# A two-layer hybrid trunk on one core: inputs laid out feature-major, the first loads reordered, the long convolution's taps in other proportions and its rows last in the projection

## The chip, the core and the metric

One core of a Trainium2 chip runs the whole program in one launch. The metric is device time in microseconds (us); the median of 3 runs of the kernel before is 2325.66 us (2324.86 to 2325.68).

## What is computed

Two layers of a decoder trunk for 256 prompt positions and 8 sample positions (264 columns in all), model width 2048, float32 in and out. Per layer:

```
z  = rmsnorm(x) @ W_in                       # columns for the groups A, B, C, D
ya = b * conv3(c * x~)                       # A: short causal convolution, taps aw, with a past state
yb = rmsnorm_head(GLA(q, k, v, log a)) * silu(r)             # B: gated linear attention, with a state
yc = silu(layernorm(conv31(glu(c1, c2)) + cb))               # C: depthwise, 31 taps cw, with a past state
yd = u * (tril(W_s) @ layernorm(gelu(v)) + b_s)              # D: spatial gating
x  = x + concat(ya, yb, yc, yd) @ W_o
x  = x + (silu(h @ W_gate) * (h @ W_up)) @ W_down            # h = rmsnorm(x), d_ff 5632
```

and a last rmsnorm. Outputs are y for prompt and sample, and the new states of the convolutions, of the GLA and of D.

## The kernel before

Everything is held feature-major: features on the 128 partitions, the 264 tokens as columns. `xs` is the residual in 16 k-tiles of 128x264; `split_x` makes from it, times the norm's gain, a high part `xh` (fp32r) and a rest `xl`. Each weight matrix is walked by `stream`: for a group of 512 output columns, k-tiles come in **chunks** of two (KC = 2). A chunk is one DMA of 512 KB into `raw` (4 buffers), a cast by ScalarE to `wh` (L293), a subtraction by VectorE to `wl` (L294; `wh` and `wl` have 3 buffers), and 4 x 2 x 3 = 24 matmuls of 264 columns on TensorE (L308 `xh`,`wh`; L309 `xl`,`wh`; L310 `xh`,`wl`). A 2048-row group is 8 chunks, 192 matmuls. In the mixer the groups run in the order c2, c1, r (528 columns), q, v, vd, u, ac, ax, ab, then four groups of the projection w_o; then the feed-forward network (FFN) runs w_gate, w_up and w_down.

Around the change:

- **Opening.** `x_prompt` lies token-major in HBM. It is loaded in four DMAs into `xp` and turned by TensorE: per k-tile two transposes of `xp` (L343) and one of the sample rows `xd` (L344) into `ps_x`, then a copy to `xs` by ScalarE (L346) or VectorE (L348). The gain is loaded as 4 rows and transposed too (L139). All of the first loads are issued by SyncE, in the order of the code: a quarter of x, the gain, the sample rows, two chunks of weights, a quarter of x, two chunks, the rest of x.
- **Small weights.** `load_rows` (L118) loads the per-feature vectors as 53 rows of 512; `prep_params` (L144) transposes them (L147) to `par`. `prep_state` transposes the past states of the two convolutions (L164, L174) and folds them into `accs` and `accA`. The spatial weights `sgr` are masked, transposed to `wst` (L469), and their first entries spread by a matmul (L472). In layer 0 this happens on GpSimd's DMA queue and in the program after c1; for layer 1 the parameters and states are loaded by SyncE and turned within layer 0's FFN.
- **The long convolution (C).** `conv_all` yields 4 x (1 + 30 + 1) = 128 steps: per 128 features one ScalarE start, 30 VectorE taps (L482, 128x256) and one tap for the samples. `step_back`, called once a chunk, issues as many steps as a rate says: 1.5 a chunk for 16 chunks, then 2.5. When the steps are used up, `fin_c` runs the LayerNorm over `cc` (its reductions by TensorE, its chain by VectorE), Silu on ScalarE (L503, with a table load) and `emit_y(8)`, which makes `yh8` (L382) and `yl8` (L383): the C rows of w_o's input.
- **The projection.** `order` (L829) says in which order its 16 k-tiles are used: D (12 to 15), B (4 to 7), C (8 to 11), A (0 to 3). The A rows `yah`, `yal` (L822, L823) are made from the group before, ab.

The instructions of each engine stand in an order that a scheduler fixes at build time; each engine runs its own in that order.

## Time and profile before

| what | value |
|---|---|
| median of 3 runs | 2325.66 us |
| the profiled execution | 2325.71 us |
| its span in the trace | 2323.8 us |
| TensorE (PE) busy | 2293.6 us, 99% |
| VectorE (DVE) busy | 1414.0 us, 61% |
| ScalarE (ACT) busy | 1019.2 us, 44% |
| DMA, mean rate | 177 GB/s |
| TensorE idle, waiting for `yh` | 11.1 us, in 2 waits |

The profiled execution is 0.05 us from the median of the runs, so sums are made against 2325.71. A matmul row's duration covers its whole way through the array, and rows overlap: what a matmul costs is the distance between the starts of neighbours. Idle time of an engine is only lost where the engine is the one that sets the end.

### The profile page before, as it was taken

How to read it: one execution, taken by the hardware profiler on the slowest of the kernel's cores; microseconds unless marked ns; L12 is line 12 of the kernel's file. 1: busy time of each engine (PE TensorE's matmuls, PEld its weight loads, DVE VectorE, ACT ScalarE, POOL GpSimd, SP SyncE). 2: the span in 40 equal slices, each digit the busy share in tenths (PEclk: the TensorE clock that was granted, in tenths of full speed). 3: DMA queues.
4: the chain of work that ended last, by engine and by line, in shares of the span. 5: the costliest groups of instructions: out<-in, count | busy, mean ns of one | idle time of the engine just before them, and what ended most of it. 6: DMA issues, size and time to landing. Idle time of an engine off the chain costs nothing.

```text
span 2323.8 us, 44164 instructions
## 1 busy us (share of the span) xinstructions
PE 2293.6 (99%) x18656; PEld 2271.3 (98%) x18656; DVE 1414.0 (61%) x2076; ACT 1019.2 (44%) x1302; POOL 71.1 (3%) x138
## 2 busy tenths in 40 slices
PE   9999999999999999999999999999999999999997
PEld 8999989999999999999999998999999999999997
DVE  6699966555655555444467998565555555554444
ACT  5644444444444444444345444444444444434333
POOL 3101000000000000000020100000000000000000
PEclk9999999999999999999999999999999999999999
DMA  8446545555555555555574555555555555555553
GB/s 243 146 155 183 172 153 187 182 181 181 180 189 182 182 182 182 179 178 180 182 202 149 174 172 169 162 179 180 181 181 189 182 182 181 182 181 174 177 177 129
DMA packets 208874, 412.44 MB, mean 177 GB/s; under 512 B 14001, under 2 KB 14067, under 8 KB 208644
## 3 DMA queue, kind: packets, MB, share of 16 engines
q1 hardware_dynamic: 204644, 400.53, 54.1%
q0 software_dynamic: 4032, 9.09, 1.5%
q8 instruction: 146, 2.39, 0.4%
q14 instruction: 52, 0.43, 0.1%
HBM read 404.25 MB, written 6.29 MB: 177 GB/s over the span
## 4 chain that ended last, share of the span: by engine, by line
PE 97%; ACT 2%; DVE 0%; issue 0%; DMA 0%; SPq 0%; DVEq 0%; ACTq 0%
PE pw L308 23%; PE pw L309 23%; PE pw L310 23%; PE pwx L308 8%; PE pwx L309 8%; PE pwx L310 8%; PE ps_lv L597 1%; PE ps_os L705 0%; ACT s L701 0%; ACT wh L293 0%; DMA raw<-in_w_in_dram 0%; PE ps_y L870 0%; ACT cc L503 0%; PE ps_sv L774 0%; PE ps_o L667 0%
## 5 line engine op out<-in xcount | busy, mean ns | idle before, releaser
L294 DVE TENSOR_TENSOR wl<-raw,wh 128x1024 fp32r<-128x1024 f32 x752 | 918.8, 1223 | 763.7 <-ACT wh L293 763.0
L293 ACT ACTIVATE wh<-raw 128x1024 fp32r<-128x1024 f32 (+1 forms) x752 | 795.7, 1060 | 1219.5 <-PE pw L309 694.2
L308 PE MATMUL pw<-xh,wh 128*128 128x264 f32 x3136 | 889.4, 286 | 1.9 <-ACT wh L293 1.7
L309 PE MATMUL pw<-xl,wh 128*128 128x264 f32 x3136 | 887.4, 285 | 0.0
L310 PE MATMUL pw<-xh,wl 128*128 128x264 f32 x3136 | 874.0, 285 | 0.1
L308 PEld LDWEIGHTS pw<-xh,wh 128*128 128x128 f32 x3136 | 590.2, 189 | 3.8 <-ACT wh L293 2.4
L309 PEld LDWEIGHTS pw<-xl,wh 128*128 128x128 f32 x3136 | 590.7, 188 | 2.3 <-issue 1.7
L310 PEld LDWEIGHTS pw<-xh,wl 128*128 128x128 f32 x3136 | 583.7, 189 | 6.9 <-issue 4.0
L308 PE MATMUL pwx<-xh,wh 128*128 128x264 f32 x960 | 272.9, 285 | 0.0
L310 PE MATMUL pwx<-xh,wl 128*128 128x264 f32 x960 | 272.2, 284 | 0.0
L309 PE MATMUL pwx<-xl,wh 128*128 128x264 f32 x960 | 272.1, 284 | 0.0
L309 PE MATMUL pw<-hl,wh 128*128 128x264 f32 x880 | 250.6, 285 | 0.0
L308 PE MATMUL pw<-hh,wh 128*128 128x264 f32 x880 | 250.1, 285 | 0.0
L310 PE MATMUL pw<-hh,wl 128*128 128x264 f32 x880 | 248.7, 285 | 0.0
L308 PEld LDWEIGHTS pwx<-xh,wh 128*128 128x128 f32 x960 | 180.8, 188 | 0.1
L310 PEld LDWEIGHTS pwx<-xh,wl 128*128 128x128 f32 x960 | 180.8, 188 | 0.0
L309 PEld LDWEIGHTS pwx<-xl,wh 128*128 128x128 f32 x960 | 180.5, 188 | 0.0
L308 PEld LDWEIGHTS pw<-hh,wh 128*128 128x128 f32 x880 | 165.8, 188 | 0.0
L309 PEld LDWEIGHTS pw<-hl,wh 128*128 128x128 f32 x880 | 165.7, 188 | 0.0
L310 PEld LDWEIGHTS pw<-hh,wl 128*128 128x128 f32 x880 | 165.1, 189 | 0.1
L309 PE MATMUL pwx<-hl,wh 128*128 128x264 f32 x528 | 150.7, 285 | 0.0
L308 PE MATMUL pwx<-hh,wh 128*128 128x264 f32 x528 | 150.2, 285 | 0.0
(311 smaller groups left out, 2259.9 us busy)
## 6 DMA issues: line engine op xcount, KB each, us to landing
raw<-in_w_gate_dram SPq DMA_DIRECT2D x176, 512.0 KB
raw<-in_w_up_dram SPq DMA_DIRECT2D x176, 512.0 KB
raw<-in_w_down_dram SPq DMA_DIRECT2D x176, 512.0 KB
raw<-in_w_in_dram SPq DMA_DIRECT2D x144, 512.0 KB
raw<-in_w_o_dram SPq DMA_DIRECT2D x64, 512.0 KB
raw<-in_w_in_dram SPq DMA_DIRECT2D x16, 528.0 KB
xp<-in_x_prompt_dram SPq DMA_DIRECT2D x4, 512.0 KB
...
```

The lines of the kernel that those rows point to most:

```text
L293: actf(wh[:, :, :ncol], r[:, :, :ncol], AF.Copy)
L294: sub = tt(out=wl, in0=r[:, :, :512], in1=wh[:, :, :512].bitcast(F32), op=ALU.subtract)
L308: mm(out=o, lhsT=a, rhs=rh[kk], start=first, stop=False)
L309: mm(out=o, lhsT=a, rhs=rl[kk], start=False, stop=False)
L310: mm(out=o, lhsT=wl[:, j, m * P:(m + 1) * P], rhs=rh[kk], start=False, stop=last)
L597: mm(out=pl[:, g * P:(g + 1) * P], lhsT=pm[:, q, blk(Tb)], rhs=qd[:, q, :, Tb * 64:Tb * 64 + 64], start=True, stop=True)
```

## The change

**Layout.** The host lays x, the per-feature vectors, the taps, the spatial weights and a second copy of the convolution states out feature-major, so each loads straight into place; x_prompt is padded to 264 columns. The transposes of x, of the gain, of the parameters, of the states and of the spatial weights leave the program, with the copies behind them. `par` now takes 11 loads of 128 short rows (8 to 496 bytes a partition).

**First loads.** SyncE issues the gain, then x in pieces of 2, 2, 4, 4, 4 k-tiles with the sample columns and chunks 2 and 3 of the weights between them; ScalarE issues chunk 0 (in two halves) and chunk 1. Chunk 0 is cast and subtracted in halves. Five small copies bring the sample columns from `xd` into `xs`. In both layers the other small loads (`small_loads`, and in layer 0 the parameters and states too) are issued after the first evacuation of c2.

**Taps and rows.** The rate is 3 steps a chunk for 8 chunks, 2.25 for 8, then 2.5. The C rows stand last in w_o's order, the A rows third.

```diff
-        back.append((conv_all(), fin_c, chain(repeat(1.5, 16), repeat(2.5))))
+        back.append((conv_all(), fin_c, chain(repeat(3, 8), repeat(2.25, 8), repeat(2.5))))
...
-        order = [o + i for o in (12, 4, 8, 0) for i in range(4)]
+        order = [o + i for o in (12, 4, 0, 8) for i in range(4)]
...
-        with tc.high_priority():
-            for i in range(4):
-                dma(out=xp[:, :, i * 512:(i + 1) * 512],
-                    in_=x_prompt[0, :, i * 512:(i + 1) * 512].rearrange("(t p) d -> p t d", p=P))
...
-        for k in range(KT):
-            ps = psm("ps_x")
-            for t in range(2):
-                transpose(ps[:, t * P:(t + 1) * P], xp[:, t, k * P:(k + 1) * P], ident)
-            transpose(ps[:, 256:264], xd[:, k * P:(k + 1) * P], ident[:NS, :NS])
...
+    with tc.high_priority():
+        xd = cst.tile([P, KT, NS], F32, tag="xd", name="xd")
+        adma = nc.scalar.dma_start
+
+        def load_x(k0, k1):
+            dma(out=xs[:, k0:k1, :], in_=x_prompt[:, k0:k1])
+
+        def load_w0(i, dma):
+            early.append(load_w(w_in[0], D_MODEL, COL["c2"], 512, i * KC, dma, KC if i == 0 else 1))
+
+        gain0 = load_gain(0)
+        load_w0(0, adma)
+        load_x(0, 2)
+        dma(out=xd, in_=x_sample)
+        load_w0(1, adma)
+        load_x(2, 4)
+        load_w0(2, dma)
+        load_x(4, 8)
+        load_w0(3, dma)
+        load_x(8, 12)
+        load_x(12, 16)
+        for k0, k1 in ((0, 2), (2, 4), (4, 8), (8, 12), (12, 16)):
+            nc.vector.tensor_copy(xs[:, k0:k1, NPT:], xd[:, k0:k1])
...
+        seen = mt("seen", [P, 1])
+        with tc.issue_after(nc.gpsimd.tensor_copy(seen, sgm[:, 0, 0:1]).ins):
+            if st is None:
+                par = load_params(l, sdma)
+                pasts = [mt("past", [P, 512], tag=tag) for tag in ("att", "t5", "t4")]
+                for i in range(3):
+                    load_state(l, i, pasts[i], sdma)
+            small_loads()
         win(COL["c1"], 512, ev_c1)
         if st is None:
-            par = prep_params(l, load_rows(l, sdma))
             build_masks()
             st = acc_tiles(l)
-            for i, tag in enumerate(("att", "t5", "t4")):
-                past = mt("past", [P, 512], tag=tag)
-                load_state(l, i, past, sdma)
-                prep_state(par, i, past, *st)
+            for i in range(3):
+                prep_state(par, i, pasts[i], *st)
...
-        psW = psm("ps_ws")
-        for h in range(H):
-            transpose(psW[:, h * P:(h + 1) * P], sgr[:, h, :], ident)
-        actf(wst.rearrange("p h i -> p (h i)"), psW, AF.Copy)
-        psw0 = psm("ps_w0")
-        mm(out=psw0[:, :H], lhsT=ones_s[0:1, :], rhs=wst[0:1, :, 0], start=True, stop=True)
```

How the instructions stand is shown at three places. The first is TensorE's opening, before (`pw` are the accumulators of the group c2):

```order
L343 MATMUL ps_x<-ident,xp 128x128 x2
L139 MATMUL ps_gain<-ident,grow 128x4 x4
L343 MATMUL ps_x<-ident,xp 128x128 x2
L344 MATMUL ps_x<-ident,xd 128x8 x2
L343 MATMUL ps_x<-ident,xp 128x128 x2
L344 MATMUL ps_x<-ident,xd 128x8
L343 MATMUL ps_x<-ident,xp 128x128 x2
L344 MATMUL ps_x<-ident,xd 128x8
L308 MATMUL pw_261<-xh,wh 128x264
L308 MATMUL pw_262<-xh,wh 128x264
L308 MATMUL pw_263<-xh,wh 128x264
L308 MATMUL pw_264<-xh,wh 128x264
```

and with the change, where line numbers have moved by one (L309, L310, L311 are the three matmuls):

```order
L309 MATMUL pw_165<-xh,wh 128x264
L309 MATMUL pw_166<-xh,wh 128x264
L309 MATMUL pw_167<-xh,wh 128x264
L309 MATMUL pw_168<-xh,wh 128x264
L310 MATMUL pw_165<-xl,wh 128x264
L311 MATMUL pw_165<-xh,wl 128x264
L309 MATMUL pw_165<-xh,wh 128x264
L310 MATMUL pw_166<-xl,wh 128x264
L311 MATMUL pw_166<-xh,wl 128x264
```

The 52 transposes ahead of and between the first matmuls are gone; the first instruction is a matmul of the stream.

The second is VectorE at the start of layer 0's projection, before. The four `wl` rows are the projection's chunks 4, 5, 6 and 7 (counted from 0), between them stands the end of the LayerNorm of C, and TensorE wants `yl8` in chunks 4 and 5:

```order
L294 TENSOR_TENSOR wl_3722<-raw_3719,wh_3721 128x1024
L190 TENSOR_TENSOR sqg_3352<-sqg_3352,rsl_3360 128x264
L191 SCALAR_TENSOR_TENSOR rsl_3360<-sqg_3352,rsl_3360 128x264
L192 TENSOR_TENSOR sqg_3352<-sqg_3347,rsl_3360 128x264
L294 TENSOR_TENSOR wl_3752<-raw_3749,wh_3751 128x1024
L193 TENSOR_TENSOR sqg_3352<-sqg_3352,rsl_3360 128x264
L194 SCALAR_TENSOR_TENSOR sqg_3352<-sqg_3352 128x264
L195 SCALAR_TENSOR_TENSOR rsl_3360<-sqg_3352,rsl_3360 128x264
L428 TENSOR_TENSOR cc_913<-cc_913,rsl_3360 128x1056
L294 TENSOR_TENSOR wl_3782<-raw_3779,wh_3781 128x1024
L383 TENSOR_TENSOR yl8_3376<-cc_913,yh8_3375 128x1056
L294 TENSOR_TENSOR wl_3812<-raw_3809,wh_3811 128x1024
```

and with the change, from the last chunk of the group ab (`wl_3439`) on; `wl_3485`, `wl_3515` and `wl_3545` are the projection's chunks 0, 1 and 2, and TensorE wants `yal` in chunks 4 and 5 and `yl8` in chunks 6 and 7:

```order
L294 TENSOR_TENSOR wl_3439<-raw_3436,wh_3438 128x1024
L434 TENSOR_TENSOR cc_796<-cc_796,rsl_2994 128x1056
L294 TENSOR_TENSOR wl_3485<-raw_3482,wh_3484 128x1024
L820 TENSOR_TENSOR ya_2629<-ya_2629,pw0_3222 128x264
L820 TENSOR_TENSOR ya_2629<-ya_2629,pw1_3223 128x264
L294 TENSOR_TENSOR wl_3515<-raw_3512,wh_3514 128x1024
L820 TENSOR_TENSOR ya_2629<-ya_2629,pw2_3224 128x264
L383 TENSOR_TENSOR yl8_3010<-cc_796,yh8_3009 128x1056
L820 TENSOR_TENSOR ya_2629<-ya_2629,pw3_3225 128x264
L822 TENSOR_TENSOR yal_3221<-ya_2629,yah_3220 128x264 x2
L294 TENSOR_TENSOR wl_3545<-raw_3542,wh_3544 128x1024
L822 TENSOR_TENSOR yal_3221<-ya_2629,yah_3220 128x264 x2
```

`yl8` stood behind the `wl` of chunk 6, two chunks after the first that reads it; now it stands behind that of chunk 1, five chunks ahead of the first that reads it. The end of its LayerNorm stood among chunks 3 to 6 and now stands ahead of chunk 0.

The third is GpSimd's queue in layer 0, before, in which the loads for the attention and the spatial gating come ahead of the states and the parameters:

```order
L393 DMA a_243<-in_gla_a_dram 16x256 x2
L395 DMA sgr<-in_sg_w_dram 128x4x128
L397 DMA sgb<-in_sg_b_dram 128x512
L403 DMA s_239<-in_state_gla_dram 64x4x128 x2
L403 DMA s_240<-in_state_gla_dram 64x4x128 x2
L403 DMA s_241<-in_state_gla_dram 64x4x128 x2
L403 DMA s_242<-in_state_gla_dram 64x4x128 x2
L433 MEMSET cext 128x4x30
L156 DMA past<-in_state_conv_c_dram 120x512 x2
L158 DMA past<-in_state_conv_a_dram 16x512
L577 MEMSET pm 128x1056
```

and with the change, from the small copy that starts it on:

```order
L460 COPY seen<-sgm 128x1
L133 DMA par_432<-in_conv_c_w_dram 128x124
L133 DMA par_432<-in_conv_a_w_dram 128x12
L133 DMA par_432<-in_gla_norm_dram 128x4
L133 DMA par_432<-in_conv_c_b_dram 128x4
L133 DMA par_432<-in_ln_c_g_dram 128x4
L133 DMA par_432<-in_ln_c_b_dram 128x4
```

The parameters now come first, behind a copy of `sgm` that waits for the end of the first group; the rest of the eleven, the three states, and only then `a2`, the spatial weights and the GLA state follow.

## Rows read from the trace of the kernel before

**Rows 1.** The page's line of engine totals: busy us, share of the span, instructions.

```profile
PE 2293.6 (99%) x18656; PEld 2271.3 (98%) x18656; DVE 1414.0 (61%) x2076; ACT 1019.2 (44%) x1302; POOL 71.1 (3%) x138
```

**Rows 2.** Busy time by stretch: from:to and its length, then busy us (instructions) of PE, PEld, DVE, ACT, POOL, the granted TensorE clock, the DMA share and GB/s. A stretch inside the feed-forward network.

```profile
500.00:1000.00 500.00, 500.00 (x4116) 499.63 (x4116) 270.89 (x335) 207.32 (x250) 0.00 (x0) 1.00 0.57 182
```

**Rows 3.** Who TensorE waited for, over the whole run: us in total, times, longest.

```profile
PE pw L308 <- ACT yh L382: 11.1, 2, 5.6
PE ps_x L343 <- DMA xp<-in_x_prompt_dram: 5.3, 1, 5.3
PE pw L308 <- ACT wh L293: 1.7, 3, 0.7
```

**Rows 4.** The opening in order of time: start us, duration us, engine, line, what, how often, and the idle time before it with what ended it.

```profile
0.81 0.47 SPq L333 DMA_DIRECT2D xp<-in_x_prompt_dram  x1
2.10 1.30 SPq L269 DMA_DIRECT2D raw<-in_w_in_dram  x2
...
5.28 0.66 PE L343 MATMUL ps_x<-ident,xp 128*128 128x128 f32 x2 [5.28 <-DMA xp<-in_x_prompt_dram]
...
7.48 1.06 ACT L293 ACTIVATE wh<-raw 128x1024 fp32r<-128x1024 f32 x1 [0.80 <-DMA raw<-in_w_in_dram]
...
9.27 1.25 PE L308 MATMUL pw<-xh,wh 128*128 128x264 f32 x4 [0.24 <-ACT xh L215]
...
12.19 1.08 PE L308 MATMUL pw<-xh,wh 128*128 128x264 f32 x4
...
20.85 0.65 PE L308 MATMUL pw<-xh,wh 128*128 128x264 f32 x4
```

**Rows 5.** Busy time by stretch, columns as in rows 2: from the start to the end of the first group, and ten us within it.

```profile
0.00:41.70 41.70, 36.18 (x244) 32.08 (x245) 26.39 (x47) 26.67 (x47) 11.41 (x27) 1.00 0.77 235
...
10.00:20.00 10.00, 10.00 (x60) 8.67 (x59) 8.53 (x17) 8.27 (x15) 0.00 (x0) 1.00 0.92 341
```

**Rows 6.** Groups of VectorE instructions from 0 to 41.7 us: count, busy us, mean ns of one, and idle time before them.

```profile
L294 DVE TENSOR_TENSOR wl<-raw,wh 128x1024 fp32r<-128x1024 f32 x10 | 12.2, 1223 | 5.5 <-ACT wh L293 5.5
L216 DVE SCALAR_TENSOR_TENSOR xl<-xs,gain,xh 128x264 fp32r<-128x264 f32 x16 | 7.4, 485 | 0.8 <-ACT xh L215 0.8
...
L348 DVE COPY xs<-ps_x 128x264 f32<-128x264 f32 x8 | 3.4, 428 | 7.2 <-PE ps_x L344 7.2
```

**Rows 7.** Groups of TensorE instructions over the whole run, columns as in rows 6: the transposes of x.

```profile
L343 PE MATMUL ps_x<-ident,xp 128*128 128x128 f32 x32 | 8.0, 339 | 5.3 <-DMA xp<-in_x_prompt_dram 5.3
...
L344 PE MATMUL ps_x<-ident,xd 8*128 8x8 f32 x16 | 3.6, 237 | 0.0
```

**Rows 8.** The chain of work that ended last, from 60 to 80 us (start us, us, what): the preparation of layer 0's small weights between the stream's matmuls.

```profile
67.69 0.38 PE ps_par L147 x4
68.07 0.97 PE ps_pc L164 x8
...
71.01 0.35 PE ps_pa L174 x4
...
73.24 0.44 PE ps_ws L469 x4
...
76.70 0.31 PE ps_w L472 x2
```

**Rows 9.** In order of time, columns as in rows 4, around the projection of layer 0 (VectorE's last tap and its last part of the A rows, then ScalarE, then TensorE) and, last, TensorE in layer 1.

```profile
275.36 0.47 DVE L482 SCALAR_TENSOR_TENSOR cc<-cext,par,cc 128x256 f32<-128x256 f32 x1
...
291.91 1.11 DVE L823 TENSOR_TENSOR yal<-ya,yah 128x264 fp32r<-128x264 f32 x3
...
302.19 1.28 ACT L503 ACT_TABLE_LOAD   x1
303.49 2.10 ACT L503 ACTIVATE cc<-cc,par 128x264 f32<-128x264 f32 x4
305.62 1.08 ACT L382 ACTIVATE yh<-cc 128x1056 fp32r<-128x1056 f32 x1
...
300.92 0.28 PE L310 MATMUL pw<-yh,wl 128*128 128x264 f32 x1
306.76 1.25 PE L308 MATMUL pw<-yh,wh 128*128 128x264 f32 x4 [5.56 <-ACT yh L382]
...
311.47 0.28 PE L309 MATMUL pw<-yl,wh 128*128 128x264 f32 x1
...
1450.21 1.03 PE L308 MATMUL pw<-yh,wh 128*128 128x264 f32 x3 [5.56 <-ACT yh L382]
```

**Rows 10.** Busy time by stretch, columns as in rows 2: the matmuls behind that wait in layer 0.

```profile
306.70:311.50 4.80, 4.70 (x20) 4.39 (x21) 1.26 (x1) 0.01 (x1) 0.00 (x0) 0.51 0.14 55
```

**Rows 11.** GpSimd's loads of the small weights: one issue in order of time (columns as in rows 4), and DMA issues of a kind with KB each and the median us from issue to landing.

```profile
44.53 0.53 POOL L123 DMA_DIRECT2D prow<-in_gla_norm_dram  x1
...
past<-in_state_conv_c_dram POOLq DMA_DIRECT2D x2, 240.0 KB, 10.5
...
prow<-in_gla_norm_dram POOLq DMA_DIRECT2D x1, 2.0 KB, 6.1
```

**Rows 12.** Busy time by stretch, columns as in rows 2: the groups r, q and v of layer 0.

```profile
65.50:96.60 31.10, 30.86 (x251) 29.19 (x251) 22.00 (x52) 13.82 (x19) 5.10 (x6) 1.00 0.47 140
96.60:122.60 26.00, 25.22 (x199) 24.24 (x198) 18.51 (x31) 21.47 (x40) 0.00 (x0) 1.00 0.45 136
122.60:153.40 30.80, 30.80 (x258) 30.28 (x257) 30.55 (x60) 12.79 (x21) 0.00 (x0) 1.00 0.51 156
```

More of the change, by code (lines that the diff above doesn't have):

```diff
@@ L131, in load_gain @@
     def load_gain(l):
-        g = tmp.tile([4, 512], F32, tag="sq", name="grow")
-        dma(out=g, in_=norm_mix[l].rearrange("(r n) -> r n", r=4))
-        return g
-    def prep_gain(l, g):
-        ps = psm("ps_gain")
-        for t in range(4):
-            transpose(ps[:, t * 4:(t + 1) * 4], g[:, t * P:(t + 1) * P], ident[:4, :4])
-        gain = cst.tile([P, 4, 4], F32, tag=f"gain{l}", name=f"gain{l}")
-        actf(gain.rearrange("p t r -> p (t r)"), ps[:, :16], AF.Copy)
-        return gain
@@ L144, in prep_params @@
-    def prep_params(l, rows):
-        ps = psm("ps_par")
-        for t in range(4):
-            transpose(ps[:, t * NROW:(t + 1) * NROW], rows[:, t * P:(t + 1) * P],
-                                ident[:NROW, :NROW])
-        par = cst.tile([P, 4, NROW], F32, tag=f"par{l}", name=f"par{l}")
-        actf(par.rearrange("p t r -> p (t r)"), ps[:, :4 * NROW], AF.Copy)
-        return par
+        g = cst.tile([P, KT], F32, tag=f"gain{l}", name=f"gain{l}")
+        keep(dma(out=g, in_=norm_mix[l]))
@@ new lines, in load_gain, with load_params, pcol @@
+        return g
+    def load_params(l, dma):
+        par = cst.tile([P, NPAR], F32, tag=f"par{l}", name=f"par{l}")
+        src = dict(cw=conv_c_w[l], aw=conv_a_w[l], gn=gla_norm[l], cb=conv_c_b[l], lcg=ln_c_g[l],
+                   lcb=ln_c_b[l], ldg=ln_d_g[l], ldb=ln_d_b[l], nf=norm_ffn[l], gb=gla_a_bias[l],
+                   fin=norm_final)
+        for n, (o, w) in PAR.items():
+            keep(dma(out=par[:, o:o + w], in_=src[n]))
+        return par
+    def pcol(par, n, i):
+        o = PAR[n][0] + i
+        return par[:, o:o + 1]
@@ L160, in prep_state @@
     def prep_state(par, i, past, accs, accA):
         if i < 2:
-            ps = psm("ps_pc")
-            for t in range(4):
-                transpose(ps[:, t * 120:(t + 1) * 120], past[:120, t * P:(t + 1) * P], ident[:120, :120])
-            pw = tmp.tile([P, 4, 4, 30], F32, tag="sq", name="pw")
-            tt(out=pw, in0=ps[:, :480].rearrange("p (t b k) -> p t b k", t=4, b=4),
-               in1=par[:, :, 0:30].unsqueeze(2).to_broadcast([P, 4, 4, 30]), op=ALU.mult)
+            pw = past[:, :480].rearrange("p (t b k) -> p t b k", t=4, b=4)
@@ L168, in prep_state @@
+            tt(out=pw, in0=pw, in1=pvec(par, "cw")[:, :, 0:30].unsqueeze(2).to_broadcast([P, 4, 4, 30]),
+               op=ALU.mult)
             a = accs[:, :, 4 * i:4 * i + 4]
             nc.vector.tensor_reduce(out=a, in_=pw, axis=mybir.AxisListType.X, op=ALU.add)
-            tt(out=a, in0=a, in1=par[:, :, 35:36].to_broadcast([P, 4, 4]), op=ALU.add)
+            tt(out=a, in0=a, in1=pvec(par, "cb").to_broadcast([P, 4, 4]), op=ALU.add)
         else:
-            psA = psm("ps_pa")
-            for t in range(4):
-                transpose(psA[:, t * 16:(t + 1) * 16], past[:16, t * P:(t + 1) * P], ident[:16, :16])
@@ L175, in prep_state @@
[L175 to L179 removed]
+            pa = past[:, :64].rearrange("p (k t b) -> p k t b", k=2, t=4)
+            aw = pvec(par, "aw")
@@ L181, in acc_tiles, with old_state @@
+            tt(out=accA, in0=pa[:, 0], in1=aw[:, :, 0:1].to_broadcast([P, 4, NS]), op=ALU.mult)
+            tt(out=pa[:, 1], in0=pa[:, 1], in1=aw[:, :, 1:2].to_broadcast([P, 4, NS]), op=ALU.mult)
+            tt(out=accA, in0=accA, in1=pa[:, 1], op=ALU.add)
+    def old_state(l, a, taps):
+        return a[l][0:NS * taps * GW].rearrange("(b t c) -> b t c", b=NS, t=taps)
     def acc_tiles(l):
@@ L264, in hybrid_trunk_kernel, with load_w @@
     early = []
-    def load_w(W, rows, col0, ncol, k0):
+    fresh = [True]
+    def load_w(W, rows, col0, ncol, k0, dma=dma, pieces=1):
         r = raw_p.tile([P, KC, 528], F32, tag="raw", name="raw")
         i = rows * col0 + k0 * P * ncol
-        dma(out=r[:, :, :ncol],
-            in_=W[i:i + KC * P * ncol].rearrange("(p k n) -> p k n", p=P, k=KC))
+        w = W[i:i + KC * P * ncol].rearrange("(p k n) -> p k n", p=P, k=KC)
+        n = KC // pieces
+        for j in range(0, KC, n):
+            dma(out=r[:, j:j + n, :ncol], in_=w[:, j:j + n])
         return r
```

156 lines of the change are left out of this document (74 added, 82 removed).

## The prediction, made before the changed kernel ran

> **What bounds the kernel now.** I read the page's totals first: TensorE is busy 99% of the span [rows 1], so only what TensorE does or waits for can move the time. Then a stretch of the FFN, for its pace: 4116 matmuls in 500 us, 0.1215 us each, at the full granted clock, with VectorE at 54% [rows 2]. The stream needs 18,048 matmuls of that kind, 2193 us; the change leaves them alone. What can go is the other 130 us. Then the table of TensorE's waits [rows 3]: 11.1 us in two waits of 5.6 for `yh`, 5.3 us at the start for x, 1.7 us for casts. Last I looked at the two places themselves: the opening [rows 4 to 6] and the projection of each layer [rows 9, 10].
>
> **The wait in the projection (undone by the new rates and row order).** In layer 0 TensorE starts its last matmul of the B rows at 300.92, and the first of the C rows at 306.76, after 5.56 us of idling for `yh` [rows 9]. What is late is one chain: the last tap of the convolution at 275.36, LayerNorm, a table load at 302.19 (1.28 us), four Silus (2.10), the cast at 305.62 (1.08). Behind it comes a second cost: from 306.70 to 311.50 the granted clock reads 0.51, the 1.2 GHz level [rows 10], and from 306.76 the 19 matmuls up to 311.47 [rows 9] took 4.71 us where 0.1215 each would be 2.31, 2.4 more. Before the fall TensorE had stood idle. From 300.92 plus one matmul to 306.76 are 5.72; so a layer loses 5.7 + 2.4 = 8.1. Layer 1 shows the same wait at 1450.21 [rows 9], so 16.2 in all.
>
> With the change the 128 steps are used up after 51 chunks instead of 58 (16 chunks at 1.5 gave 24, the other 104 need 42; now 8 x 3 + 8 x 2.25 give 42, the other 86 need 35), and in the built order VectorE's last tap stands 10 chunks earlier and `yl8` 5 chunks earlier. A chunk is 24 x 0.1215 = 2.92 us, so 5 chunks are 14.6 us: `yh8` and `yl8` move from about 307 to about 292. The need for them moves the other way, two chunks later, from 301.0 to 306.9. Either part alone would do, the row order just so (5.8 against 5.7); together they leave some 14 us. The A rows take the place: the last of `yal` starts at 291.91 and takes 1.11 [rows 9], and they are needed at 301.0. That is 8 us of slack, and VectorE has less to do there. I take the whole 16.2; at worst the A rows wait instead and half is left, at best 16.4.
>
> **The opening.** TensorE begins at 5.28 with transposes, when the first 512 KB of x have landed; the first matmul of the stream is at 9.27, behind the landing of the first weights at 7.48 [rows 4]; the first group of 192 is done at 41.7 (244 instructions less the 52 transposes) [rows 5]. At 0.1215 each it would need 23.3. The rest is 9.3 of lead, then the transposes put in between (48 on x, 11.6 us of overlapping durations [rows 7]), and the low clock: at 12.19 four matmuls are 0.22 apart, at 20.85 they are 0.12 apart [rows 4], that is the lower and the upper level; ahead of the rise TensorE had done transposes and matmuls with holes.
>
> Now the first matmul needs the gain (8 KB), two k-tiles of x (264 KB) and both halves of chunk 0 (512 KB), 784 KB. Before, 512 KB of x were there at 5.28 and the sample rows, gain and first weights, 584 KB more, at 7.48, 265 KB a us. At that pace 784 KB are there at 5.28 + 272/265 = 6.3. Half a cast (0.53), then the first `xh` (0.5) give a first matmul at 7.3. ScalarE's three new issues (0.65 each by SyncE's [rows 4]) and its table load end at 4.1, under the landing. Add 23.3, add the 2.4 that the low clock cost behind the wait above, add 0.5 for feeding: 33.5, or 8.2 earlier. Feeding holds if VectorE keeps pace: 8 `wl` (1.22) and 16 `xl` (0.485) [rows 6] and twelve additions for the norm at 0.43 to 0.58 make some 23 us against 25.7 of TensorE; the 8 copies of 0.43 are gone, and five copies of the sample columns, each below 0.43, come. DMA moved 341 GB/s in this part [rows 5]; x and four chunks, 4.3 MB, are there by about 18. Bounds: a first matmul at 6.0 and half the clock cost, 30.5 (11.2 earlier); a first matmul no earlier than 9.27 and 3 us of waits for `wl`, 38.0 (3.7 earlier).
>
> The weights of chunks 0 and 1 come from ScalarE's queue. The rows show one issuer and a DMA share of 0.92 [rows 5], so I count only fewer bytes ahead, 2.0 us of the lead. The Trainium skill (DMA: Bandwidth & Descriptors, "Issuing engines are not separate DMA queues") says that transfers from several engines share the same 16 DMA engines and only issue time is saved. By that alone the lead would shrink by the 1.3 us by which the first weights are issued earlier, and the sum below would be 0.7 higher; no row here has two issuers in the opening.
>
> **The small transposes.** Parameters, states and spatial weights cost TensorE 0.38 + 0.97 + 0.35 + 0.44 + 0.31 = 2.45 us of the chain in layer 0 [rows 8]; the same instructions run once more for layer 1, so 4.9 (4.3 to 5.9, if gaps of neighbours or whole durations count). Of ScalarE's copies behind them some stood in front of casts; of the 1.7 us in which TensorE waited for casts [rows 3] I give 0.4 (0 to 1). The loads for layer 1, 12 issues by SyncE instead of 13 within the FFN, cost nothing: four `raw` buffers, 11.7 us of TensorE's work, cover them, and if they did not, it would be an issue of some 0.5 each.
>
> **What it adds.** In r and q VectorE gets 38 taps instead of 22 by the built order, 16 x 0.40 (taps follow one another at that distance) = 6.4 us more, in 57.1 us where it is busy 40.5 [rows 12]. It fits on the sum; but in q TensorE is already short of 0.8 us, waiting for a cast, and in v VectorE is busy 30.6 of 30.8. I take 1.0 for both layers (0 to 5). In layer 0 GpSimd issues parameters and states only after the first group: from 33, 14 issues of 0.53 end at 40.5, and the states land 6.1 to 10.5 later [rows 11], at 46.5 to 51. VectorE wants them behind the `wl` of c1's seventh chunk, which TensorE reaches at 33.5 + 6 x 2.92 = 51 and VectorE one or two chunks ahead, at 45 to 48. So it may stand up to 6 us, with `wl` of the next chunks queued behind; two finished chunks, 5.8 us, cover that. I count it within the 1.0.
>
> **Sum.** 2325.71 - 16.2 - 8.2 - 4.9 - 0.4 + 1.0 = 2297.0. The profiled execution is 0.05 us from the median 2325.66, so the forecast stands for the median: **2297.0 us**, 1.2% less. The forecast's own range is 2291 to 2303. A change under 0.2% (4.7 us) could not be told from none.
>
> **Rivals.**
> - *The opening is fed no faster* (the worst bound above): c2 ends at 38.0 instead of 33.5, 2301.5. For it: VectorE and ScalarE were busy 8.5 and 8.3 of ten us there [rows 5], and the `xl` of the last four k-tiles wait for the last piece of x. Against: their copies from `ps_x` are gone.
> - *VectorE becomes the bound in r, q and v.* If the 6.4 us of taps find no free place, `wl` is late by that in each layer: 2 x 6.4 more, less the 1.0 counted, 2309. For it: 30.6 of 30.8 in v. Against: 9 us free in r, 7.5 in q [rows 12], and the built order gives v 10 taps instead of 14.
> - *The wait does not go, it changes rows.* `yal` or `yl8` still comes late by half of what it was: 2305. Against it are 8 and 14 us of slack.
> - *Slower: the small loads hold everything.* The layer-0 states come last of 14 loads, 11 of them of 128 short rows, down to 8 bytes. If each had to land before the next is issued, at 6.1 for the eleven and 10.5 for the states [rows 11], the last would be there at 33 + 67 + 32 = 132. VectorE stands from 46 on, TensorE runs dry at 52: 80 us lost and 2.4 of low clock, 2379. It is slower than before once TensorE loses more than the 29.7 gained and 4.7, so from a landing at about 52 + 34 = 86. Against: before, loads of this queue were issued 0.5 apart while others were in flight. The Trainium skill (DMA: Bandwidth & Descriptors, Specifications) wants 512 bytes a transfer and says that below this the engine does a read-modify-write; no row here shows loads of 128 such pieces.
>
> **How the numbers follow.** Forecast 0.73, opening 0.09, VectorE 0.11, changed rows 0.04, slower 0.03. The range 2290 to 2308 takes in the forecast's own, the first and third rivals and the nearer half of the second; it leaves out 2309 and beyond, the slower case and a better opening, some 0.15. Faster by over 0.2%: 0.96 (all but the slower case and a part of the second rival in which several waits add up, 0.01); within 0.2%: 0.01; slower: 0.03.
>
> **What would show it.** Right: TensorE's table of waits has no `yh` and no `yal` at the projection, and the granted clock stays at 1.00 there; the first matmul at about 7.3 and c1's first at about 33.5; the projection of layer 0 begins some 12 us earlier than 288.9. Wrong: a new wait for `wl` or `wh` of several us in c1, r or q, above all one that ends with the landing of `past`; or a first group that ends later than 38.

## The result, and the profile of the changed kernel

| | us | ratio to before |
|---|---|---|
| before, median of 4 runs on the same chip | 2325.67 (2324.86 to 2327.01) | |
| changed, median of 4 runs | 2298.49 (2297.37 to 2300.40) | 0.9883 [0.9866, 0.9901] |
| predicted | 2297.0 (2290 to 2308) | |

27.2 us went; 28.7 were predicted. The profiled execution took 2299.30 us, with a span of 2297.3; by spans it is 26.5 less than before.

TensorE first, since it sets the end. The page's totals (busy us, share, instructions) answer to [rows 1]: 96 instructions fewer on TensorE, the transposes of x and gain (52) and twice the 22 small ones. VectorE and ScalarE are as busy as before.

```profile
PE 2275.0 (99%) x18560; PEld 2258.8 (98%) x18560; DVE 1412.3 (61%) x2074; ACT 1015.4 (44%) x1288; POOL 70.8 (3%) x140
```

Who TensorE waited for (us in total, times, longest), against [rows 3]:

```profile
PE pw L309 <- ACT xh L210: 6.5, 1, 6.5
PE pw L309 <- ACT wh L293: 4.1, 4, 2.0
PE ps_y L869 <- DVE xg L846: 0.3, 1, 0.3
```

The two waits for `yh` are gone and no other row of the projection took their place. The 6.5 is the start. The waits for casts grew: four of them, 4.1 us, the longest 2.0, where before three took 1.7, the longest 0.7. One stands in the opening (0.53, at 21.64), one in r of layer 0 (0.85), one in the q group of each layer (0.81 and 1.96).

**The opening** in order of time (start, duration, engine, line, what; then the idle time before it), against [rows 4]:

```profile
0.81 1.52 ACTq L268 DMA_DIRECT2D raw<-in_w_in_dram  x3
...
3.98 0.63 ACT L293 ACTIVATE wh<-raw 128x512 fp32r<-128x512 f32 x1 [0.33 <-DMA raw<-in_w_in_dram]
5.27 0.63 ACT L293 ACTIVATE wh<-raw 128x512 fp32r<-128x512 f32 x1 [0.66 <-DMA raw<-in_w_in_dram]
5.91 0.92 ACT L210 ACTIVATE xh<-xs,gain 128x264 fp32r<-128x264 f32 x2
...
6.47 1.25 PE L309 MATMUL pw<-xh,wh 128*128 128x264 f32 x4 [6.47 <-ACT xh L210]
...
8.89 1.06 ACT L293 ACTIVATE wh<-raw 128x1024 fp32r<-128x1024 f32 x1 [1.53 <-DMA raw<-in_w_in_dram]
...
13.63 1.74 ACT L210 ACTIVATE xh<-xs,gain 128x264 fp32r<-128x264 f32 x4 [1.39 <-DVE xs L350]
```

The first matmul of the stream starts at 6.47 instead of 9.27. Then ScalarE stands twice, 1.53 us for weights to land and 1.39 for a copy of sample columns that stands behind a `wl` on VectorE (12.28 to 13.50). The DMA share is 0.91 from 10 to 20 us (columns as in rows 2, against [rows 5]). TensorE itself is busy in that stretch; its matmuls are 0.22 apart up to 12.4 and 0.12 from there on, though the granted clock reads 1.00. It reads 1.00 in [rows 5] too, so the low clock that the prediction sees in the opening is read from distances, not from that column.

```profile
10.00:20.00 10.00, 10.00 (x75) 10.00 (x75) 9.73 (x22) 8.61 (x18) 0.00 (x0) 1.00 0.91 335
```

**The projection of layer 0**, against [rows 9]:

```profile
274.29 1.28 ACT L502 ACT_TABLE_LOAD   x1
...
278.55 1.07 ACT L382 ACTIVATE yh<-cc 128x1056 fp32r<-128x1056 f32 x1
...
280.16 1.25 DVE L383 TENSOR_TENSOR yl<-cc,yh 128x1056 fp32r<-128x1056 f32 x1
...
283.49 0.77 DVE L822 TENSOR_TENSOR yal<-ya,yah 128x264 fp32r<-128x264 f32 x2
...
290.65 0.28 PE L309 MATMUL pw<-yah,wh 128*128 128x264 f32 x1
...
296.52 0.28 PE L309 MATMUL pw<-yh,wh 128*128 128x264 f32 x1
```

`yl8` is ready at 281.4 and needed at 296.5, the A rows at 284.3 and 290.7: 15 and 6 us of slack. TensorE's matmuls stay 0.12 apart throughout, at a granted clock of 1.00.

**The q group of layer 1**, ScalarE and then TensorE:

```profile
1224.22 0.48 ACT L530 ACTIVATE absy<-ps_pre,par 128x264 f32<-128x264 f32 x1 [0.30 <-DVE mn L529]
1226.07 1.06 ACT L293 ACTIVATE wh<-raw 128x1024 fp32r<-128x1024 f32 x1 [1.37 <-PE pw L310]
1227.04 0.47 ACT L530 ACTIVATE absy<-ps_pre,par 128x264 f32<-128x264 f32 x1
1227.52 1.28 ACT L531 ACT_TABLE_LOAD   x1
...
1229.48 1.28 ACT L532 ACT_TABLE_LOAD   x1
1230.77 0.65 ACT L532 ACTIVATE absy<-absy 128x528 f32<-128x528 f32 x1
1231.32 1.05 ACT L293 ACTIVATE wh<-raw 128x1024 fp32r<-128x1024 f32 x1
1232.39 1.28 ACT L632 ACT_TABLE_LOAD   x1
...
1233.93 4.79 ACT L700 ACTIVATE s<-s,as 128x128 f32<-128x128 f32 x16
1238.63 1.04 ACT L293 ACTIVATE wh<-raw 128x1024 fp32r<-128x1024 f32 x1
...
1239.72 0.39 PE L309 MATMUL pw<-xh,wh 128*128 128x264 f32 x1 [1.96 <-ACT wh L293]
```

Read it by the casts (L293): they start at 1226.07, 1231.32, 1238.63. The middle gap holds two table loads, the last a third table load and sixteen scalings of the GLA state (L700). TensorE has used up its stock of casts and idles 1.96 us. Behind that the granted clock reads 0.50, the 1.2 GHz level, as one stretch shows: 18 matmuls in 3.40 us, where 28 would fit at 0.1215.

```profile
1241.30:1244.70 3.40, 3.40 (x18) 3.40 (x17) 3.02 (x5) 2.04 (x3) 0.00 (x0) 0.50 0.49 154
```

**Where the time went.** Below, the times between the first matmuls of successive groups of the stream, taken from both traces:

| term | before | changed | difference | predicted |
|---|---|---|---|---|
| end of the first group (c2) of layer 0 | 41.72 | 33.75 | -8.0 | -8.2 |
| r of layer 0; r of layer 1; FFN of layer 0 | 31.18; 28.22; 773.30 | 28.79; 27.67; 771.34 | -4.9 | -4.9 small transposes |
| c1 of layer 1 | 23.69 | 23.33 | -0.4 | (-0.4 casts, in no named group) |
| first projection group, layers 0 and 1 | 32.02; 31.91 | 23.44; 23.41 | -17.1 | -16.2 |
| q to ab, layer 0 | 192.26 | 192.66 | +0.4 | +1.0 new costs, with the next row |
| q to ab, layer 1 | 192.22 | 195.34 | +3.1 | |

These sum to -26.9; the other groups add 0.3, and the spans differ by 26.5. Of the 3.1, the q group alone is 2.75 (25.90 to 28.65). Of the 17.1, 0.9 was not the wait: the last reduction of the convolution's LayerNorm (`ps_var`) ran inside the projection before, 0.45 us of TensorE's time a layer, and now runs in ax. So the wait was worth 16.2, and what was added from q to ab is 2.6.

The -4.9 and the -0.4 hide two larger numbers. Four of the transposes of the spatial weights stood in c1 of layer 1 (L469 in the trace before, at 1211.54), and none of the three waits for casts did, so the -0.4 belongs to the transposes. And r of layer 0 carries a new wait: it took 28.79 here, but 27.67 in e3 and e5, which have the same matmuls there and no wait, as r of layer 1 took. So the small transposes were worth 6.4 (3.51 in r of layer 0, where TensorE had waited 0.21 for a cast before, 1.96 in layer 0's FFN, 0.36 and 0.55 in c1 and r of layer 1), and 1.1 was lost again behind a cast that came late because its weights landed late (ScalarE, TensorE, then DMA issues between 40 and 62 us with KB each and median us to landing):

```profile
60.27 1.08 ACT L293 ACTIVATE wh<-raw 128x1056 fp32r<-128x1056 f32 x1 [3.79 <-DMA raw<-in_w_in_dram]
...
61.41 0.39 PE L309 MATMUL pw<-xh,wh 128*128 128x264 f32 x1 [0.85 <-ACT wh L293]
...
raw<-in_w_in_dram SPq DMA_DIRECT2D x6, 528.0 KB, 7.2
s<-in_state_gla_dram POOLq DMA_DIRECT2D x8, 128.0 KB, 8.7
```

Weights took 7.2 us to land there, against 3.8 to 4.0 within the FFN (500 to 1000 us), beside 2.1 MB of GpSimd's small loads, which the change issues behind the first group. That these loads delay the weights is read from the times and was not tried by itself.

### The profile page after: what moved, and what is told of

The parts are those of the page before. It is cut to its first block, busy times and chain, and to the rows that moved or that the text cites. A ratio compares the mean times of both kernels' runs of the same rounds, so it can differ in the third digit from the quotient of the medians.

```text
span 2297.3 us, 43967 instructions
## 1 busy us (share of the span) xinstructions
PE 2275.0 (99%) x18560; PEld 2258.8 (98%) x18560; DVE 1412.3 (61%) x2074; ACT 1015.4 (44%) x1288; POOL 70.8 (3%) x140
## 5 line engine op out<-in xcount | busy, mean ns | idle before, releaser
L294 DVE TENSOR_TENSOR wl<-raw,wh 128x1024 fp32r<-128x1024 f32 (+1 forms) x753 | 920.1, 1223 | 749.2 <-ACT wh L293 748.0
L293 ACT ACTIVATE wh<-raw 128x1024 fp32r<-128x1024 f32 (+2 forms) x753 | 796.2, 1059 | 1206.6 <-PE pw L310 670.7
L309 PE MATMUL pw<-xh,wh 128*128 128x264 f32 x3136 | 891.2, 286 | 10.6 <-ACT xh L210 6.5
L310 PE MATMUL pw<-xl,wh 128*128 128x264 f32 x3136 | 889.5, 285 | 0.0
L311 PE MATMUL pw<-xh,wl 128*128 128x264 f32 x3136 | 876.5, 286 | 0.1
L309 PEld LDWEIGHTS pw<-xh,wh 128*128 128x128 f32 x3136 | 592.0, 189 | 16.1 <-ACT xh L210 6.5
L310 PEld LDWEIGHTS pw<-xl,wh 128*128 128x128 f32 x3136 | 592.2, 189 | 2.2 <-issue 1.7
L311 PEld LDWEIGHTS pw<-xh,wl 128*128 128x128 f32 x3136 | 585.7, 189 | 3.2 <-issue 2.0
L309 PE MATMUL pwx<-xh,wh 128*128 128x264 f32 x960 | 273.1, 284 | 0.0
L311 PE MATMUL pwx<-xh,wl 128*128 128x264 f32 x960 | 272.8, 284 | 0.0
L310 PE MATMUL pwx<-xl,wh 128*128 128x264 f32 x960 | 272.5, 284 | 0.0
L310 PE MATMUL pw<-hl,wh 128*128 128x264 f32 x880 | 250.9, 286 | 0.0
L309 PE MATMUL pw<-hh,wh 128*128 128x264 f32 x880 | 250.3, 285 | 0.0
L311 PE MATMUL pw<-hh,wl 128*128 128x264 f32 x880 | 248.9, 285 | 0.0
L309 PEld LDWEIGHTS pwx<-xh,wh 128*128 128x128 f32 x960 | 181.1, 189 | 0.0
L311 PEld LDWEIGHTS pwx<-xh,wl 128*128 128x128 f32 x960 | 181.0, 189 | 0.0
L310 PEld LDWEIGHTS pwx<-xl,wh 128*128 128x128 f32 x960 | 180.6, 188 | 0.0
L309 PEld LDWEIGHTS pw<-hh,wh 128*128 128x128 f32 x880 | 165.9, 189 | 0.0
L310 PEld LDWEIGHTS pw<-hl,wh 128*128 128x128 f32 x880 | 165.8, 188 | 0.0
L311 PEld LDWEIGHTS pw<-hh,wl 128*128 128x128 f32 x880 | 165.3, 189 | 0.1
L310 PE MATMUL pwx<-hl,wh 128*128 128x264 f32 x528 | 150.7, 286 | 0.0
L309 PE MATMUL pwx<-hh,wh 128*128 128x264 f32 x528 | 150.3, 285 | 0.0
```

The costliest lines, as they stand in the source:

```text
L293: actf(wh[:, j, :ncol], r[:, j, :ncol], AF.Copy)
L294: sub = tt(out=wl[:, j, :], in0=r[:, j, :512], in1=wh[:, j, :512].bitcast(F32), op=ALU.subtract)
L309: mm(out=o, lhsT=a, rhs=rh[kk], start=first, stop=False)
L310: mm(out=o, lhsT=a, rhs=rl[kk], start=False, stop=False)
L311: mm(out=o, lhsT=wl[:, j, m * P:(m + 1) * P], rhs=rh[kk], start=False, stop=last)
```

## The experiments

Each run was timed beside the kernel before on its chip (medians 2325.07 to 2326.45), and is told by its own median; group times are from its one profiled execution. All edits but that of e4 start from the changed kernel.

**1. Rates, rows, or both.** Three kernels take one or both of the tail's edits back (the first edit in e1 and e3, the second in e2 and e3); e4 puts only the tail's edits on the kernel before.

```diff
-chain(repeat(3, 8), repeat(2.25, 8), repeat(2.5))
+chain(repeat(1.5, 16), repeat(2.5))
...
-order = [o + i for o in (12, 4, 0, 8) for i in range(4)]
+order = [o + i for o in (12, 4, 8, 0) for i in range(4)]
```

e1, old rates with the new rows:

> The changed kernel with the old tap rates (1.5, then 2.5 steps a chunk), its new row order kept. Theory (either half of the change covers the wait by itself): the C rows are ready at about the old 306.7 and wanted at 306.9, so at most 0.5 us of waiting a layer, o0 at 23.4 to 24 us instead of 32.0; the group q of layer 1 is no longer short of casts and falls from 28.7 back to 25.9. In all 2296 to 2300 against 2298.5 of the changed kernel. Rival (the rates do the work, the row order nothing): the wait comes back at the later rows, 2 to 6 us of idling and 2.4 of low clock a layer, 2307 to 2315.

Measured 2299.06 (2298.45 to 2303.36), first projection group 25.33. The wait is of the size expected, 0.5 us a layer (the waits of e1, columns as above), but the group is 1.9 longer than 23.4. 0.45 of that is `ps_var`, which is back in the projection. The other 1.5 lie between 295.94 and 298.41, where eight distances of matmuls take 2.47 us instead of 0.97: the wait for `yh`, a cast that ScalarE could run only behind `yh` (0.2 idle), and the first matmuls after each.

```profile
PE pw L309 <- ACT wh L293: 3.6, 6, 1.1
PE pw L309 <- ACT yh L382: 1.0, 2, 0.5
```

e2, new rates with the old rows:

> The changed kernel with the old row order (C rows third, A rows last), its new tap rates kept. Theory: the C rows are ready near 292 on the old clock of layer 0 and wanted at 301, so no wait: o0 at 23.4 us, 2298.5 like the changed kernel, within 1.5. Rival (the row order does the work): the Silu and yh come after the group ab has ended, the wait comes back with 2 to 6 us and the low clock, 2306 to 2315.

Measured 2298.21 (2296.95 to 2299.18), no wait for `yh`, first projection group 23.41: the rates alone remove all of it.

e3, both old:

> The changed kernel with both the old rates and the old row order; layout and loads new. Theory: the wait for yh comes back whole, o0 at 32.0 us in both layers, 17.1 us over the changed kernel, less the 2.7 that q of layer 1 regains: 2313 to 2316. Rival (the wait was due to the transposes and the late loads, not to rates and rows): o0 stays at 23.4, 2296 to 2299.

Measured 2311.85 (2310.93 to 2313.02). The mechanism is as expected: the wait is back at its old size, with the low clock behind it at 292.1 to 298.9 (TensorE in e3, as in rows 9):

```profile
295.67 1.25 PE L309 MATMUL pw<-yh,wh 128*128 128x264 f32 x4 [5.56 <-ACT yh L382]
```

The time is 1 us below the expected range: the first projection groups took 31.31 and 31.36, not 32.0. TensorE's idle time is the same 5.56, but in layer 0 the matmuls behind it were at the low clock for 3.2 us, where before it was 4.8 [rows 10]. With the old rates q of layer 1 is back at 25.94.

e4, the kernel before with the new rates and rows:

> The kernel before with only the two lines of the tail changed (new rates, new row order); layout and loads old. Theory: both waits of 5.6 us and their low clock go, 17.1 us, less up to 2.7 if q of layer 1 loses as in the changed kernel: 2308.5 to 2311.5. If q's loss comes from the new layout, 2308.5 and q at 25.9. Rival (the rates cost VectorE elsewhere what they give here): above 2315.

Measured 2311.92 (2311.36 to 2313.51), 13.7 less than before and a little above the range. The first projection group is 23.5 in layer 0 and 23.4 in layer 1, so the 17.1 are there. Against them stand the q group of layer 0, 1.1 longer behind a wait of 1.90 for a cast, and an opening that ended at 44.11 in the profiled execution, 2.4 later than before, its matmuls 0.22 apart up to 19.4, where before they were 0.12 apart from 15.4 at the latest. Why that came later there I can't say; q of layer 1 stays at 25.91, so the new rates alone do not make it late; the other three runs are 1.2 to 2.2 us shorter. What e3 saves (13.7) and what e4 saves (13.7) sum to 27.4, against 27.2 for the whole change: the tail is half of it, opening and small weights the other half, and within the spread of the runs the two simply add.

**2. What the order and the two issuers of the first loads are worth.** e5 keeps the layout and takes before's order, chunk 0 in one piece, all issued by SyncE (the first part; unchanged lines and the one copy of sample columns less are not shown); e6 only lets SyncE issue the first weights (the second part).

```diff
-fresh = [True]
+fresh = []
...
-early.append(load_w(w_in[0], D_MODEL, COL["c2"], 512, i * KC, dma, KC if i == 0 else 1))
+early.append(load_w(w_in[0], D_MODEL, COL["c2"], 512, i * KC, dma, 1))
...
-gain0 = load_gain(0)
-load_w0(0, adma)
-load_x(0, 2)
-dma(out=xd, in_=x_sample)
-load_w0(1, adma)
-load_x(2, 4)
-load_w0(2, dma)
-load_x(4, 8)
+load_x(0, 4)
+gain0 = load_gain(0)
+dma(out=xd, in_=x_sample)
+load_w0(0, dma)
+load_w0(1, dma)
+load_x(4, 8)
+load_w0(2, dma)
...
-adma = nc.scalar.dma_start
+adma = nc.sync.dma_start
```

> The changed kernel with the feature-major layout kept and the first loads in the order of the kernel before, all issued by SyncE: four k-tiles of x, gain, sample columns, chunks 0 and 1, four k-tiles, chunks 2 and 3, the rest; chunk 0 whole. Theory (layout and order each give a part): 1112 KB stand ahead of the first matmul, as before, so it starts at about 9.0 instead of 6.5; the group c2 ends at 36.3 instead of 33.75, 2301 in all. Rival 1 (the layout alone does it, since the casts of c2 bound it anyway): c2 ends within 0.7 of 33.75, 2298.5 to 2299. Rival 2 (the order does it): c2 ends above 39, 2304 and more.

Measured 2298.88 (2298.76 to 2299.62): first matmul 10.09, end of the first group 35.86 as expected, but the time is 2 us below. In this execution q of layer 1 took 27.13 instead of 28.65, though TensorE's wait there is the same 1.96: the clock did not fall behind it. r of layer 0 was 1.1 shorter as well, without the wait of 0.85. So this run could not tell what the order is worth; e11 does.

> The changed kernel with the weights of chunks 0 and 1 issued by SyncE too, in the order of the code. Theory (only the bytes ahead count): the two halves of chunk 0 and x are issued some 0.8 to 1.5 later, first matmul at 7.3 to 8.0, c2 ends at 34.5 to 35.2, 2299 to 2300. Rival (two issuing engines bring more bandwidth): first matmul above 8.5, c2 ends above 36, 2301 and more. Second rival (issue time was hidden by the data): first matmul at 6.5, no difference.

Measured 2297.62 (2297.13 to 2298.55): first matmul 7.54, 1.1 later than with two issuers, end of the first group 33.20, not later at all. The other traces agree: with one issuer (e6, and e9 and e10 below) the first matmul is at 7.38 to 7.99 and the group ends at 33.20 to 33.84, with two (the changed kernel, e1, e2, e3, e7, e8, e12) at 6.47 to 6.91 and 32.30 to 34.12. A single issuer costs the start and nothing at the end that the spread of executions would show. That is what the Trainium skill says (DMA: Bandwidth & Descriptors, "Issuing engines are not separate DMA queues"): a second issuer saves only the issue time. The trace agrees, with 1.1 us at the first matmul and none at the end of the group.

**3. The late cast in q.** Two suspects: ScalarE's scalings of the GLA state, and VectorE's taps. e7 moves the sixteen scalings to GpSimd (first part); e8 lowers the middle rate (second part).

```diff
-actf(s0[:, j, :], s0[:, j, :], AF.Copy, scale=as_[:, q, b:b + 1])
+nc.gpsimd.tensor_scalar(out=s0[:, j, :], in0=s0[:, j, :], scalar1=as_[:, q, b:b + 1], scalar2=None, op0=ALU.mult)
...
-chain(repeat(3, 8), repeat(2.25, 8), repeat(2.5))
+chain(repeat(3, 8), repeat(1.5, 8), repeat(2.5))
```

> The changed kernel with the sixteen scalings of the GLA state in each layer done by GpSimd instead of ScalarE. Theory (q's waits come from ScalarE, which does the sixteen in one piece of 4.8 us between two casts): no wait of TensorE for wh in q, q at about 24.7 in both layers instead of 25.95 and 28.65, the clock does not fall at 1241, 2292 to 2295. Rival (VectorE's extra taps make q late): q unchanged, 2298.5. Third way: GpSimd is slow or takes VectorE's port, the state comes late to the attention, above 2300.

Measured 2295.81 (2294.34 to 2297.63). 0.8 above what was expected. q is 24.59 and 24.94, better than in either kernel (1.4 and 3.7 less than in the changed one), but the groups v to ab take 1.1 and 1.4 more: the scalings take 15 us on GpSimd (e7, in order of time) where ScalarE took 4.79, and TensorE's table has a new wait of 1.1 us for `vb` at `ps_os` (L704).

```profile
1231.72 15.06 POOL L700 TENSOR_SCALAR s<-s,as 128x128 f32<-128x128 f32 x16 [34.67 <-ACT as L632]
```

> The changed kernel with the rates 3 for eight chunks, 1.5 for eight, then 2.5, that is fewer taps in q (14 in the built order instead of 19). Theory (ScalarE's piece of 4.8 us makes q late): q of layer 1 stays above 28, 2298 to 2299; the last tap comes 4 chunks later, which o0 does not feel (23.4). Rival (VectorE's taps make q late): q of layer 1 falls to 25.9, 2295.5 to 2296.

Measured 2295.96 (2295.47 to 2296.72), q of layer 1 25.94, no fall of the clock: the rival of that run. Either suspect alone, taken away, ends the long wait (e8 keeps 0.75 of it), so neither is the whole cause.

**4. The two remedies together, and the order again.** Three kernels with the middle rate 1.5: with one issuer (e9), with one issuer and the scalings on GpSimd (e10), with the old load order (e11).

> The changed kernel with two edits that were each tried alone: the middle rate 1.5 instead of 2.25, and SyncE instead of ScalarE issuing the first weights. Theory: the gain of the rate (2.5 us: the layer-1 q group 25.9 instead of 28.7) lies at another place than what the issuer does in the opening, so it stays whole, and the issuer is worth nothing at the end of the first group (33.2 to 33.8): 2295.0 to 2296.2. Rival: the issuer's 1.1 us later first matmul costs time after all and was hidden in the earlier run by a luckier q: 2296.5 to 2297.5.

Measured 2296.48 (2294.91 to 2297.99), q 25.94, end of the first group 33.84. It lies 0.3 above the theory's range and at the edge of the rival's; against e8 (2295.96) the issuer is not told from nothing.

> As the run before (middle rate 1.5, SyncE issues the first weights), and the 16 scalings of the GLA state run on GpSimd as well. Theory: both remedies of the late cast in q take away one and the same wait, so together they give no more than the better one in q (24.6 to 25.0), and GpSimd's scalings lengthen v and vd as when they were tried alone (vd about 36): 2294.5 to 2296. Rival: they add up, the second giving another 2.5 us: 2292.5 to 2293.5.

Measured 2293.35 (2292.37 to 2295.34), ratio 0.9862 [0.9847, 0.9877]. The rival of that run holds: they add up, 3.1 below e9 and 2.5 below e7. My theory took the wait for one and the same. But at 25.94 q still holds a wait of 0.75 for a cast, in each layer; without the scalings it is gone and q takes 24.58 in both, and v to ab give back only 0.35 and 0.06, where in e7 they gave back 1.1 and 1.4. That is 2.3 of the 3.1; 0.7 is c1 of layer 1, where TensorE waited 0.51 for a `wl` in e9. Of the kernels run this is the quickest, 5.1 below the changed one.

> The changed kernel with the load order of before (a quarter of x, gain, sample rows, chunk 0 and 1 whole, and so on, all by SyncE; layout feature-major) and the middle rate 1.5, so that the q group of layer 1 doesn't hide what the order is worth. Theory: the new order is worth the 2.1 us at the end of the first group that the profiles showed (35.9 against 33.8), and the earlier run of the old order gave that back by a shorter q (27.1 against 28.7); with q short in both kernels it shows in the time: 2297.5 to 2298.5, the end of the first group at about 35.9. Rival: what the opening gains comes back as a longer r group of layer 0 (28.8 against 27.7), whatever q does: 2295.8 to 2296.8.

Measured 2298.25 (2297.21 to 2299.09), end of the first group 35.30, against 2295.96 in e8 and 2296.48 in e9. The theory holds: the new order, with the halves of chunk 0 and the two issuers that e11 takes back as well, is worth about 2 us (1.8 to 2.3 by the medians); the rest of the opening's 8 is the layout.

**5. Which taps.** In q of the changed kernel VectorE's two `mn` (L529) are parted (in order of time):

```profile
1223.69 0.49 DVE L529 TENSOR_SCALAR mn<-ps_pre,par 128x264 f32<-128x264 f32 x1 [1.39 <-PE ps_pre L528]
1224.10 1.22 DVE L294 TENSOR_TENSOR wl<-raw,wh 128x1024 fp32r<-128x1024 f32 x1
1225.23 0.49 DVE L529 TENSOR_SCALAR mn<-ps_pre,par 128x264 f32<-128x264 f32 x1
```

In e8 they are a pair, and ScalarE has a cast between its two table loads. e12 lowers the rate only for the two chunks in which they run; after r and q 42 steps are done, as in the changed kernel.

```diff
-chain(repeat(3, 8), repeat(2.25, 8), repeat(2.5))
+chain(repeat(3, 8), repeat(1.5, 2), repeat(2.5))
```

> The changed kernel with the rates 3 a chunk for 8 chunks, 1.5 for 2, then 2.5: only the first two chunks of the q group have fewer steps, and after the 16 chunks of r and q 42 steps are done as in the changed kernel. Theory: the wait in the layer-1 q group comes from one place, VectorE's two mn (L529) being parted by a wl, so that ScalarE runs both table loads (L531, L532) ahead of a cast; with the pair together the cast comes 1.2 us sooner: the wait falls from 1.96 to about 0.75, the granted clock stays up, the q group takes 25.9, and the time is 2295.5 to 2297.0 with no fewer taps in q. Rival: it is the number of taps in r and q that makes VectorE late; with 42 again the wait stays near 2.0, the q group takes 27.1 to 28.7 and the time stays 2297.5 to 2299.5.

Measured 2295.42 (2294.67 to 2296.58), ratio 0.9866 [0.985, 0.9883]. ScalarE, VectorE and TensorE in q of layer 1:

```profile
1223.32 0.93 ACT L530 ACTIVATE absy<-ps_pre,par 128x264 f32<-128x264 f32 x2 [0.18 <-DVE mn L529]
1224.27 1.28 ACT L531 ACT_TABLE_LOAD   x1
...
1226.11 1.05 ACT L293 ACTIVATE wh<-raw 128x1024 fp32r<-128x1024 f32 x1
1227.18 1.28 ACT L532 ACT_TABLE_LOAD   x1
...
1229.02 1.04 ACT L293 ACTIVATE wh<-raw 128x1024 fp32r<-128x1024 f32 x1
...
1236.64 1.04 ACT L293 ACTIVATE wh<-raw 128x1024 fp32r<-128x1024 f32 x1
...
1222.79 0.94 DVE L529 TENSOR_SCALAR mn<-ps_pre,par 128x264 f32<-128x264 f32 x2 [1.23 <-PE ps_pre L528]
...
1237.74 0.39 PE L309 MATMUL pw<-xh,wh 128*128 128x264 f32 x1 [0.76 <-ACT wh L293]
```

The `mn` stand together, the cast at 1226.11 lies between the two table loads, the wait is 0.76 as expected, q takes 25.93, and the clock stays up. With the same number of taps done by the end of q, 3.1 us are gone by the medians, 2.7 of them in q by the profiled executions. So it is not that VectorE or ScalarE has too much to do in q: the wait comes from the order in which their instructions stand, which a change of rate moved.

That the one `wl` between the two `mn` decides it is not shown: e12 moved ScalarE's cast along with it. In q of layer 0 of e4 a tap and no `wl` stands between the two `mn`, which are 0.81 apart, both `absy` run before the cast, and TensorE waits all the same. Common to both cases is ScalarE's order, in e4 (TensorE last):

```profile
106.27 1.06 ACT L293 ACTIVATE wh<-raw 128x1024 fp32r<-128x1024 f32 x1 [0.56 <-PE pw L309]
107.34 1.28 ACT L532 ACT_TABLE_LOAD   x1
...
109.30 1.28 ACT L533 ACT_TABLE_LOAD   x1
...
111.15 1.04 ACT L293 ACTIVATE wh<-raw 128x1024 fp32r<-128x1024 f32 x1
...
119.85 0.39 PE L308 MATMUL pw<-xh,wh 128*128 128x264 f32 x1 [1.90 <-ACT wh L293]
```

In all fourteen traces, wherever both table loads stand between two casts and ScalarE does the scalings, the wait is 1.90 or 1.96 (five q groups); wherever a cast stands between the loads, it is 0.74 to 0.82; and without the scalings (e7, e10) there is none.

## Why the prediction held, and where it was off

- **The wait in the projection: right, to 0.1.** 16.2 predicted, 17.1 measured, of which 0.9 is the LayerNorm's reduction that changed groups. The agreement to 0.1 is in part luck: in e3 the same wait came back for 15.8, 14.9 without the reduction, since the low clock behind it was shorter. The slack was 15 us for the C rows (14 predicted) and 6 for the A rows (8). "Either part alone would do, the row order just so" is half right: the rates do (e2), the row order leaves 0.5 us of wait and 1.9 of group time a layer (e1). The margin of 0.1 us taken from the sum was less than the sum is good for.
- **The opening: right in sum, wrong in two parts.** First matmul 6.47, not 7.3; end of the group at 33.75, not 33.5. The time from the one to the other is 27.3 where 26.2 was counted (23.3, 2.4 of low clock, 0.5 for feeding). "I count only fewer bytes ahead, 2.0 us of the lead" is the step that failed: with one issuer the lead falls by 1.7 (9.27 to 7.54), with two by 1.1 more. By the distances of the matmuls the 27.3 are 23.4 at 0.122 each, 2.5 more for those 0.22 apart, 0.3 behind the first one, and 1.1 at a cast that came late at 21.64 and the matmuls behind it; that cast stood behind eight `xh` on ScalarE, when the DMA share was down to 0.51 (18 to 20 us). With one issuer less was lost at late casts, 0 to 0.4 us in e6, e9 and e10, against 0.6 to 1.6 in the seven kernels with two. So what the issue gained at the start was taken again within the group.
- **The small transposes and the casts: right in sum by luck.** 5.3 was predicted for both and 5.3 is what the groups lost. But the transposes were worth 6.4, above the range of 4.3 to 5.9; the 0.4 for casts had the wrong sign, since the waits for casts grew from 1.7 to 4.1 us; and 1.1 was lost in r of layer 0. That the 6.4 belongs to those instructions was read from the places, not tried by itself.
- **What it adds: the term that was mis-sized.** 1.0 for both layers was predicted (0 to 5); 3.7 is measured, 1.1 in r of layer 0 and 2.6 from q to ab, the latter all in q of layer 1. The prediction named the place (TensorE in q short of a cast) and not the path: it looked at whether VectorE's taps fit on the sum, and they do; but the added steps changed the order of VectorE's instructions, and ScalarE's table loads came to stand together in front of a cast. The rival "VectorE becomes the bound" would have shown waits for `wl`; TensorE's table of the changed kernel has none. It was a ScalarE chain that turned late.
- **The small loads after the first group: right on their own landing.** 14 issues of parameters and states run on GpSimd from 33.28 to 41.2; the two states of the long convolution land 4.1 us after issue (median) and VectorE begins on them at 48.96 without a wait. The slower rival is out: the loads of 128 short rows were issued one behind the other, and TensorE and VectorE did not wait for them to land. What the prediction did not weigh is that the loads of this queue run beside those of weights; the late cast in r of layer 0 points to that. The first and third rivals did not show.

```profile
33.28 0.72 POOL L133 DMA_DIRECT2D par<-in_conv_c_w_dram  x1
...
39.63 1.07 POOL L151 DMA_DIRECT2D past<-in_state_conv_c_dram  x2
...
past<-in_state_conv_c_dram POOLq DMA_DIRECT2D x2, 240.0 KB, 4.1
...
48.96 0.65 DVE L160 TENSOR_TENSOR past<-past,par 128x480 f32<-128x480 f32 x1
```

- **Off without a reason: the sign for layer 0.** The projection of layer 0 begins at 278.93, 9.95 earlier than the 288.88 of before; the prediction said some 12. Its own terms give 8.2 + 2.45 = 10.7; the 12 did not follow from them.

The medians differ from the forecast by 1.5 us. By spans it is 2.2: 2.7 from the new cost, 0.4 from the casts, 0.2 from the opening and 0.3 from other groups, less 1.5 that the transposes gave more than was counted; the profiled execution is 0.8 above the median of its runs. So the forecast came nearer than its terms.
